# The last projection of a hybrid attention block as seven products of quarters in place of eight

## The chip, the cores and the metric

The kernel runs on one core of a Trainium2 chip. The metric is device time of one execution in microseconds; the runs that are shown are executions of the same program, and their median is the time of the kernel.

## The reference

One decoder block on x of 1024 tokens by 1024 features, in fp32: a sparse attention branch and a gated linear recurrence, each projected to 1024 features, are merged by gates to m, and m is projected by w_out and added to x. The change concerns the last product alone, m (1024 x 1024) by w_out (1024 x 1024), and the making of m.

```python
def reference(x, norm_gain, w_in, ..., w_proj_a, w_proj_b, w_out):
    for _layer in range(DEPTH):
        h = rms_norm(x, norm_gain)
        proj = h @ w_in
        q, kv_all, g_nsa, br_gate, u_lru, g_lru, merge_g = jnp.split(proj, split_idx, axis=-1)
        ...
        y_a = nsa_mixer(q, ...)
        y_a = (y_a * jax.nn.silu(g_nsa)) @ w_proj_a
        y_b = rglru_mixer(u_lru, ...)
        y_b = (y_b * jax.nn.silu(g_lru)) @ w_proj_b
        gate_a, gate_b = jnp.split(merge_g, N_BRANCHES, axis=-1)
        m = jax.nn.sigmoid(gate_a) * y_a + jax.nn.sigmoid(gate_b) * y_b
        x = x + m @ w_out
    return x
```

## The kernel before

All large products keep fp32's precision by parts: an operand is split into hi (rounded to a format that TensorE takes at full speed) and lo (the rest), and a product is three: hi by hi, hi by lo, lo by hi. `mm3` issues the three matmuls (lines 170 to 172). A split is two instructions: ScalarE copies to hi, and VectorE or GpSimd subtracts hi from the fp32 value to get lo. A scheduler orders each engine's own queue by priority, which is the order of the code, with some steps marked as more urgent; each engine then works its queue in that order, and waits at an instruction whose inputs or place aren't ready.

The stages are: the projections of h, the recurrence, the attention with side products between its steps, then the tail. In the tail `merge(half, ...)` makes m transposed, for 512 tokens at a time: `merge(1, ...)` first, then `merge(0, ...)`. For each of eight blocks m of 128 features it projects the attention's output into a PSUM bank (mm3), VectorE multiplies by the gate out of PSUM (line 780), adds the other mixer's part, loaded to SBUF (line 784), ScalarE writes hi (line 786) and VectorE lo (line 787). So `mT[half, m]` holds 128 features of 512 tokens, hi in its first 512 columns and lo in its last.

`out_weights(nh)` loads the weights of 512 output columns in four pieces of 512 KB (lines 1000 and 176), through two buffers named `w_raw`; ScalarE (line 1002) and VectorE (line 1003) split each in two pieces of 512 columns. The places for the first half are the attention's buffers `p_slc`, `p_win`, `ph` and `pl`; those for the second are the buffers `big_l0` and `big_l1`, once the projection of the attention no longer needs them.

The last loop takes eight blocks of 128 tokens for each half of the output's columns. A block is 24 matmuls of 512 columns into one PSUM bank (8 pieces of the inner dimension by 3), VectorE adds x to it (line 1027), and SyncE's queue stores it (line 1028). The very last block is done as two of 256 columns. GpSimd's queue (G in the code) is in use up to the end of the attention, for splits (line 185), masks and sums, and issues the stores named L95. The names in rows are those of the buffers: `kTs` and `bias` are two buffers whose pieces serve in turn as blocks of 512 columns in the tail; `st`, `ev`, `eo` and `ep` are small blocks of 512 columns; `t` and `big_h` hold mT.

Of the kernel before, what the change touches and what calls it, by code (L numbers as in the profile page):

```python
# [31 lines left out]
NEV = 3  # L32
# [18 lines left out]
# where the p of the units after the fourth lie in one tile  # L51
# [35 lines left out]
def _build(ctx, tc, A, out, dbg):  # L87
# [39 lines left out]
    def ps_f(most):  # L127
        """the banks of the products beside the attention; more of them after it"""
        if tail:
            return next(tail[0])()[:, 0:most]  # L130
        return (ps("ps_f", PF) if PF else ps_s())[:, 0:min(most, FW)]
# [4 lines left out]
    def rotation():  # L136
        """the banks of scores and of those products, in turn"""
        n = PB[0] + PF
        return itertools.cycle([(lambda: ps("ps_f", PF)) if k * PF // n != (k + 1) * PF // n else ps_s for k in range(n)])
# [6 lines left out]
    # after the attention: banks and blocks that it held  # L146
# [32 lines left out]
    def wsplit(raw, k, into=None, E=None):  # L179
        """hi and lo parts of 1024 weights per partition, as [128, k, n]"""  # L180
# [61 lines left out]
    kcT = K.tile([128, 2, 2, 64], FR, name="kcT")  # L242
    vcc = K.tile([128, 2, 2, 64], FR, name="vcc")
    # the norms of heads are taken of sums, not means: (sum + 64 eps) ** -0.5. The queries' scale takes
    # the missing factor 8, the keys' gain gets it
# [7 lines left out]
    def chunk_half(o, wh, wl, half):  # L253
        """o [128, 512] = w^T h^T, tokens of one half"""
# [44 lines left out]
    # -4 softplus(-lambda): log1p by the series of atanh  # L299
# [19 lines left out]
    yb = DR.tile([4, 128, S], FT, name="yb")  # L319

    def lru(n):
# [32 lines left out]
        # t = tanh(log_a / 2): a = (1 + t) / (1 - t), sqrt(1 - a^2) = 2 sqrt(-t) / (1 - t)  # L354
# [18 lines left out]
    def compress():  # L373
# [7 lines left out]
        for j in range(2):  # L381
# [3 lines left out]
            for g in range(2):  # L385
# [3 lines left out]
                for b in range(2):  # L389
                    # token 16 (c + b) + 2 l  # L390
# [78 lines left out]
    def qkv(g):  # L469
        """q and the keys and values of both branches, tokens on partitions"""  # L470
# [36 lines left out]
        # sigmoid(z) = (1 + tanh(z / 2)) / 2: tanh is in every table that the neighbours use  # L507
# [14 lines left out]
    def prep(g, tb, e=None):  # L522
        """norms, the split in two parts and the transposes of one token block"""
# [54 lines left out]
    def scores(g, i, br, st):  # L578
        """p [128, 4 heads, n keys] and the jobs that fill it, one per head; those of the first
        branch fill the compressed branch's p too"""  # L580
# [22 lines left out]
        def job(h):  # L603
# [4 lines left out]
            for c0, c1 in zip(cuts, cuts[1:]):  # L608
# [4 lines left out]
                # the columns of s by where their bias comes from  # L613
# [47 lines left out]
    def tr(p, c0):  # L661
        """p^T of 128 keys of the four heads, in two parts"""
# [10 lines left out]
    def tr_c(pc):  # L673
        """p^T of the compressed keys of the four heads: high parts over low parts"""
# [31 lines left out]
    def units(g):  # L706
        """(jobs, steps) of each unit; a step is a transpose and the product that follows it"""
# [35 lines left out]
    def gated(half, y1):  # L743
        """y_a^T, gated, in two parts, tokens of one half"""
# [14 lines left out]

    def merge(half, pa, m1, ya):  # L760
        """(y_a, projected, + the other mixer's part)^T, tokens of one half"""
        tk = slice(half * 512, (half + 1) * 512)
        for m in range(8):
# [20 lines left out]
            (V if tail else G).tensor_tensor(out=gt, in0=gt, in1=bt, op=OP.add)  # L784
            mt = m1[:, m] if m1 is not None else ta(FR)
            C.activation(mt[:, 0:512], gt, AF.Copy, scale=0.5)
            V.scalar_tensor_tensor(out=mt[:, 512:], in0=gt, scalar=0.5, in1=f(mt[:, 0:512]),
# [319 lines left out]
```

## Time and profile before

| | |
|---|---|
| Runs shown | 908.63, 909.22, 911.12 us; median 909.22 |
| Profiled execution | span 908.0 us; its own time is given as this span alone |
| TensorE busy | 874.2 us (96%) in 5670 matmuls |
| VectorE busy | 573.3 us (63%) in 1626 instructions |
| ScalarE busy | 439.1 us (48%) |
| GpSimd busy | 300.6 us (33%) in 339 instructions |
| DMA | 92.49 MB, mean 102 GB/s |

Busy times are sums over the whole span; an engine that is idle on average may still be the one that is waited for in a stage. PE is TensorE, DVE is VectorE, ACT is ScalarE, POOL is GpSimd, SP (SPq) is SyncE's queue, which issues transfers. A matmul's recorded duration overlaps that of the next, so that its cost is read from the distance between starts. "[2.80 <-DVE bg L500]" means that the engine was idle for 2.80 us before this instruction, until VectorE's instruction of line 500 that wrote bg was done. PEclk is the clock that TensorE was granted: 1.00 is 2.4 GHz, 0.50 is 1.2.

### The profile page before, as it was taken

The numbers are of one execution on the slowest core, as the hardware profiler recorded it, in microseconds if no ns is written. First come the engines' busy times: TensorE is split into PE (matmuls) and PEld (weight loads), VectorE is DVE, ScalarE is ACT, GpSimd is POOL, SyncE is SP. The second block draws the span as 40 slices with busy tenths as digits, with TensorE's granted clock in tenths as the row PEclk, the third lists the DMA queues.
The fourth block names the chain that finished last, engine by engine and source line by source line (L and its number), as shares of the span: only waits on it lengthen the run. The fifth ranks groups of instructions, "written<-read, shape, count | busy, mean of one in ns | idle before, by whom it ended". The sixth has DMA issues, their size and how long they took to land.

```text
span 908.0 us, 15833 instructions
## 1 busy us (share of the span) xinstructions
PE 874.2 (96%) x5670; PEld 781.0 (86%) x5670; DVE 573.3 (63%) x1626; ACT 439.1 (48%) x1159; POOL 300.6 (33%) x339
## 2 busy tenths in 40 slices
PE   4999999989899999999999999999999899999998
PEld 3678878889899999999999998999999877888887
DVE  5642778897722447475687867677777886784111
ACT  6421434645523548575566666566667663321000
POOL 4122233169622325252455553243233421000000
PEclk9999999999999999999999999999999999999999
DMA  9215321121312112122121232111113469983111
GB/s 340 64 49 139 131 95 55 55 82 48 117 48 82 59 48 74 52 86 69 55 66 65 77 102 75 47 54 60 46 42 119 132 202 331 336 270 119 70 70 47
DMA packets 45519, 92.49 MB, mean 102 GB/s; under 512 B 6896, under 2 KB 12704, under 8 KB 45440
## 3 DMA queue, kind: packets, MB, share of 16 engines
q1 hardware_dynamic: 44480, 88.33, 28.9%
q0 software_dynamic: 960, 3.15, 0.9%
q8 instruction: 44, 0.72, 0.3%
q14 instruction: 35, 0.29, 0.1%
HBM read 64.15 MB, written 25.21 MB: 98 GB/s over the span
## 4 chain that ended last, share of the span: by engine, by line
PE 80%; DVE 7%; DMA 4%; POOL 4%; issue 2%; ACT 2%; SPq 0%; DVEq 0%; ACTq 0%; POOLq 0%
PE ps_f L170 9%; PE ps_f L171 9%; PE ps_f L172 9%; PE ps_s L612 7%; PE ps_s L170 7%; PE ps_s L171 7%; PE ps_s L172 7%; PE ps_t L665 6%; PE ps_t L170 4%; PE ps_t L171 4%; PE ps_t L172 4%; PE ps_o L690 3%; PE ps_o L689 3%; POOL ss L193 1%; DVE sq L536 1%
## 5 line engine op out<-in xcount | busy, mean ns | idle before, releaser
L171 PE MATMUL ps_f<-big_l,w_hi 128*128 128x256 f32 (+1 forms) x700 | 200.3, 286 | 0.0
L170 PE MATMUL ps_f<-big_h,w_hi 128*128 128x256 f32 (+1 forms) x664 | 193.8, 292 | 1.0 <-ACT ev L829 0.8
L172 PE MATMUL ps_f<-big_h,w_lo 128*128 128x256 f32 (+1 forms) x664 | 189.4, 285 | 0.0
L171 PEld LDWEIGHTS ps_f<-big_l,w_hi 128*128 128x128 f32 x700 | 131.9, 188 | 2.1
L170 PEld LDWEIGHTS ps_f<-big_h,w_hi 128*128 128x128 f32 x664 | 125.6, 189 | 4.1 <-ACT ev L829 2.3
L172 PEld LDWEIGHTS ps_f<-big_h,w_lo 128*128 128x128 f32 x664 | 125.4, 189 | 1.6
L670 DVE TENSOR_TENSOR pl<-ps_t,ph 128x512 fp32r<-128x512 f32 x132 | 90.4, 686 | 47.5 <-ACT ph L669 46.0
L185 POOL TENSOR_TENSOR w_lo<-w_raw,w_hi 128x1024 fp32r<-128x1024 f32 x33 | 80.7, 2448 | 102.1 <-ACT w_hi L184 101.7
L669 ACT ACTIVATE ph<-ps_t 128x512 fp32r<-128x512 f32 x132 | 78.1, 599 | 48.8 <-PE ps_t L665 45.6
L650 POOL TENSOR_SCALAR p_slc<-p_slc,mx,bg 128x384 f32<-128x384 f32 (+7 forms) x88 | 68.7, 786 | 89.5 <-DVE mx L649 34.8
L646 ACT ACTIVATE p_slc<-ps_s,mx 128x256 f32<-128x256 f32 (+5 forms) x128 | 68.1, 541 | 24.1 <-DVE mx L644 18.6
L171 PE MATMUL ps_s<-big_l,w_hi 128*128 128x512 f32 (+1 forms) x184 | 73.8, 401 | 0.0
L184 ACT ACTIVATE w_hi<-w_raw 128x1024 fp32r<-128x1024 f32 (+1 forms) x40 | 42.4, 1062 | 43.6 <-PE ps_f L171 17.5
L636 DVE TENSOR_REDUCE mx<-ps_s 128x1 f32<-128x256 f32 (+5 forms) x120 | 50.9, 436 | 11.0 <-PE ps_s L612 9.3
L170 PE MATMUL ps_s<-big_h,w_hi 128*128 128x512 f32 x136 | 55.3, 408 | 2.5 <-ACT big_h L237 2.5
L689 PE MATMUL ps_o<-ph,t 128*128 128x512 f32 x132 | 55.7, 422 | 0.0
L650 POOL TENSOR_SCALAR p_win<-p_win,mx,bg 128x640 f32<-128x640 f32 (+1 forms) x40 | 34.7, 869 | 59.3 <-DVE mx L649 25.5
L665 PE MATMUL ps_t<-ident_r,p_slc 128*128 128x128 f32 x336 | 54.2, 273 | 0.0
L612 PE MATMUL ps_s<-kTs,t 128*128 128x512 f32 (+4 forms) x224 | 53.0, 349 | 0.6 <-ACT pc L621 0.3
L172 PE MATMUL ps_s<-big_h,w_lo 128*128 128x512 f32 x136 | 53.5, 397 | 0.0
L641 DVE CUSTOM_DVE_ANT_0 ps_s<-ps_s,bias 128x256 f32<-128x256 f32 (+1 forms) x128 | 52.5, 417 | 1.4 <-PE ps_s L612 0.3
L690 PE MATMUL ps_o<-pl,t 128*128 128x512 f32 x132 | 53.2, 403 | 0.0
(331 smaller groups left out, 2213.3 us busy)
## 6 DMA issues: line engine op xcount, KB each, us to landing
w_raw<-in_w_in SPq DMA_DIRECT2D x30, 512.0 KB
t<-in_x SPq DMA_DIRECT2D x8, 512.0 KB
gb<-ev SPq DMA_DIRECT2D x16, 256.0 KB
ga<-ev SPq DMA_DIRECT2D x16, 256.0 KB
w_raw<-in_w_out SPq DMA_DIRECT2D x8, 512.0 KB
st<-mb SPq DMA_DIRECT2D x16, 256.0 KB
w_raw<-in_w_tok SPq DMA_DIRECT2D x6, 524.0 KB
ev<-in_cw SPq DMA_DIRECT2D x8, 256.0 KB
```

The lines of the kernel that those rows point to most:

```text
L170: T.matmul(o, lh, rh, start=first, stop=False)
L171: T.matmul(o, lh, rl, start=False, stop=False)
L172: T.matmul(o, ll, rh, start=False, stop=last)
L185: (E or (V if tail else G)).tensor_tensor(out=lo, in0=raw, in1=f(hi), op=OP.subtract)
L612: T.matmul(s, qT[h][:, i * 128:(i + 1) * 128], rhs, start=(hl == 0), stop=(hl == 1))
L646: C.activation(p[:, h, k0:k1], sv, AF.Exp, bias=mx[:, 6:7], accum_out=mx[:, 7 + j:8 + j])
L650: G.tensor_scalar(out=p[:, h], in0=p[:, h], scalar1=mx[:, 9:10], scalar2=bg[:, g, i, 4 * (br + 1) + h:4 * (br + 1) + h + 1], op0=OP.mult, ...
L665: ins = T.transpose(pt[:, h * 128:(h + 1) * 128], p[h][:, c0:c0 + 128], ident)
L669: C.activation(ph, pt, AF.Copy)
L670: V.tensor_tensor(out=pl, in0=pt, in1=f(ph), op=OP.subtract)
L689: T.matmul(o, vf, pp[0], start=first, stop=False)
L690: T.matmul(o, vf, pp[1], start=False, stop=False)
```

## The change

m is cut in four quarters of 512 x 512, A00 and A01 (the first 512 tokens, `mT[0, 0:4]` and `mT[0, 4:8]`) and A10 and A11 (the last 512), w_out likewise in B00, B01, B10 and B11. Seven products make the output:

- S1 = A10 + A11, S2 = S1 - A00, S3 = A11 - S2, S4 = A01 - S2 of m; T1 = B01 - B00, T3 = B11 - B01, T2 = B00 + T3, and T4 = B10 - (B11 - T1) of the weights.
- In TensorE's order: A11 T4, S1 T1, A00 B00, A01 B10, S2 T2, S3 T3, S4 B11. Each is four blocks of 128 tokens with 12 matmuls of 512 columns; the last block's are of 256.
- Outputs add up in SBUF: x00 gets A00 B00 and A01 B10; d (tokens of the second half, columns of the first) gets A11 T4, A00 B00, S2 T2 and S3 T3; e gets S1 T1, A00 B00 and S2 T2, and is added to x11 (with S3 T3) and x01 (with S4 B11).

TensorE's matmuls for this go from 360 of 512 columns and 48 of 256 to 324 and 24. The sums are done in fp32 and split afterwards by `w_parts` (lines 1028 and 1029) and `parts_of` (762 and 763). Who does the sums: S1 is added by VectorE within `merge(1, ...)` (lines 797 and 802, through the blocks `a10`), S2 by VectorE (lines 1096 to 1098), S3 and S4 by GpSimd (`less`, lines 1104 and 1105, 16 instructions of 512 columns), and the sums of weights by GpSimd (lines 1037, 1040, 1042, 1052 and 1053, 10 instructions of 1024 columns, whose two inputs and output lie in SBUF in the buffers `w_raw` and `w_hi`). Outputs are added by VectorE out of PSUM (line 1080) except the first of e, which ScalarE copies (line 1114), and the addition of e, in SBUF, to x11 and x01. Quarters of w_out are loaded more than once: 20 loads of 512 KB (line 1022) for 8.

The diff, cut to its core:

```diff
+    def parts_of(o, i, scale):
+        C.activation(o[:, 0:512], i, AF.Copy, scale=scale)
+        V.scalar_tensor_tensor(out=o[:, 512:], in0=i, scalar=scale, in1=f(o[:, 0:512]), op0=OP.mult, op1=OP.subtract)
...
+        if half:
+            a10 = [K.tile([128, 512], FT, name="ev", bufs=NEV) for _ in range(3)] + [te2("ep")]
...
-            (V if tail else G).tensor_tensor(out=gt, in0=gt, in1=bt, op=OP.add)
+            E = V if tail else G
             mt = m1[:, m] if m1 is not None else ta(FR)
-            C.activation(mt[:, 0:512], gt, AF.Copy, scale=0.5)
-            V.scalar_tensor_tensor(out=mt[:, 512:], in0=gt, scalar=0.5, in1=f(mt[:, 0:512]),
-                                   op0=OP.mult, op1=OP.subtract)
             mT[half, m] = mt
+            if half and m < 4:
+                E.tensor_tensor(out=a10[m], in0=gt, in1=bt, op=OP.add)
+            else:
+                E.tensor_tensor(out=gt, in0=gt, in1=bt, op=OP.add)
+                parts_of(mt, gt, 0.5)
+            if half and m > 3:
+                E.tensor_tensor(out=gt, in0=gt, in1=a10[m - 4], op=OP.add)
+                parts_of(mT[half, m - 4], gt, 0.5)
             yield w * 0.00126
...
-        wo0.extend(out_weights(0))
...
+        wo.update(zip(("T4", "T1"), sums_a()))
         for _ in merge(0, pa, None, gated_y[0]):
             pass
 
-    def out_weights(nh):
...
-        for kp in range(4):
-            raw = wload(A["w_out"][nh, kp])
...
-        for nh in range(2):
-            wo = wo0 if nh == 0 else out_weights(1)
-            for tb in (4, 5, 6, 7, 0, 1, 2, 3):
...
-                        mm3(s[:, d], mt[:, th], mt[:, tl], wo[kc][0][:, d], wo[kc][1][:, d], kc == 0, kc == 7)
-                    V.tensor_tensor(out=xt[:, d], in0=s[:, d], in1=xt[:, d], op=OP.add)
-                    (dma, nc.gpsimd.dma_start, nc.scalar.dma_start)[DO](out[t, nh * 512 + c0:nh * 512 + c0 + w], xt[:, d])
+    wo = {}
+    def room_a():
+        ws, ww = fr(p_slc()), fr(p_win())
+        w = [(x[:, k * 1024:k * 1024 + 512], x[:, k * 1024 + 512:(k + 1) * 1024]) for x, n_ in ((ws, 4), (ww, 2)) for k in range(n_)]
+        w += [[K.tile([128, 512], FR, name=n_, bufs={"ph": 2, "pl": NPL}[n_]) for n_ in ("ph", "pl")] for _ in range(2)]
+        return w[0:4], w[4:8]
+    def room_b(h):
+        w = t_l(h, 8)
+        return [(w[:, k], w[:, 4 + k]) for k in range(4)]
+    def w_raw(kh, nh, kp, n_="w_raw"):
+        raw = f(ST.tile([128, WTOK], FR if n_ != "w_raw" else FT, name=n_, bufs=2))[:, 0:1024]
+        dma(raw, A["w_out"][nh, 2 * kh + kp])
+        return raw
+    def w_parts(o, raw, E=None):
+        for k in range(2):
+            r = raw[:, k * 512:(k + 1) * 512]
+            C.activation(o[k][0], r, AF.Copy)
+            (E or V).tensor_tensor(out=o[k][1], in0=r, in1=f(o[k][0]), op=OP.subtract)
+    def sums_a():
+        t4, t1 = room_a()
+        for kp in range(2):
+            r = slice(2 * kp, 2 * kp + 2)
+            b00, b01 = w_raw(0, 0, kp), w_raw(0, 1, kp)
+            G.tensor_tensor(out=b01, in0=b01, in1=b00, op=OP.subtract)
+            w_parts(t1[r], b01)
+            b11 = w_raw(1, 1, kp)
+            G.tensor_tensor(out=b11, in0=b11, in1=b01, op=OP.subtract)
+            b10 = w_raw(1, 0, kp)
+            G.tensor_tensor(out=b10, in0=b10, in1=b11, op=OP.subtract)
+            w_parts(t4[r], b10)
+        return t4, t1
+    def sums_b():
+        t2, t3 = room_a()
+        for kp in range(2):
+            r = slice(2 * kp, 2 * kp + 2)
+            b01, b11, b00 = w_raw(0, 1, kp), w_raw(1, 1, kp, "w_hi"), w_raw(0, 0, kp, ("w_hi", "w_raw")[kp])
+            G.tensor_tensor(out=b11, in0=b11, in1=b01, op=OP.subtract)
+            G.tensor_tensor(out=b00, in0=b00, in1=b11, op=OP.add)
+            w_parts(t2[r], b00)
+            w_parts(t3[r], b11)
+        return t2, t3
+    def quarter(h, kh, nh):
+        o = room_b(h)
+        for kp in range(2):
+            w_parts(o[2 * kp:2 * kp + 2], w_raw(kh, nh, kp))
+        return o
+    def last_projection():
+        banks = itertools.cycle([ps_t, ps_s, ps_s, ps_t, ps_s, ps_s])
+        S1, A11 = [[mT[1, k + c] for k in range(4)] for c in (0, 4)]
+        A00, A01 = [[mT[0, k + c] for k in range(4)] for c in (0, 4)]
+        def prod(a, b, j, c=slice(0, 512), s=None):
+            s = next(banks)() if s is None else s
+            th, tl = slice(j * 128, (j + 1) * 128), slice(512 + j * 128, 512 + (j + 1) * 128)
+            for k in range(4):
+                mm3(s[:, c], a[k][:, th], a[k][:, tl], b[k][0][:, c], b[k][1][:, c], k == 0, k == 3)
+            return s
+        def quads(t):
+            return [t[:, j * 512:(j + 1) * 512] for j in range(4)]
+        def add(o, s):
+            V.tensor_tensor(out=o, in0=s, in1=o, op=OP.add)
+        def rows_of(ap, mh, nh, j):
+            return ap[mh * 512 + j * 128:mh * 512 + (j + 1) * 128, nh * 512:(nh + 1) * 512]
+        def x_of(o, mh, nh):
+            for j in range(4):
+                dma(o[j], rows_of(A["x"], mh, nh, j))
+            return o
+        hi, lo = slice(0, 512), slice(512, 1024)
+        wo["B00"] = quarter(0, 0, 0)
+        S2f = []
+        for k in range(4):
+            t = K.tile([128, 512], FT, name="ev", bufs=NEV) if k < NEV else te2("eo")
+            V.tensor_tensor(out=t, in0=f(S1[k][:, hi]), in1=f(A00[k][:, hi]), op=OP.subtract)
+            V.tensor_tensor(out=t, in0=t, in1=f(A00[k][:, lo]), op=OP.subtract)
+            V.tensor_tensor(out=t, in0=t, in1=f(S1[k][:, lo]), op=OP.add)
+            S2f.append(t)
+        def less(a, k):
+            t = t_st()
+            G.tensor_tensor(out=t, in0=f(a[:, hi]), in1=S2f[k], op=OP.subtract)
+            G.tensor_tensor(out=t, in0=t, in1=f(a[:, lo]), op=OP.add)
+            return t
+        d = x_of([te() for _ in range(4)], 1, 0)
+        for j in range(4):
+            add(d[j], prod(A11, wo["T4"], j))
+        wo["B10"] = quarter(1, 1, 0)
+        e = [te() for _ in range(4)]
+        for j in range(4):
+            C.activation(e[j], prod(S1, wo["T1"], j), AF.Copy)
+        for k in range(4):
+            parts_of(A11[k], less(A11[k], k), 1.0)
+        for k in range(4):
+            parts_of(S1[k], S2f[k], 1.0)
+        S3, S2 = A11, S1
+        wo["T2"], wo["T3"] = sums_b()
+        x00 = [f(ST.tile([128, WTOK], FR, name="w_lo", bufs=2)) for _ in range(2)]
+        x00 = x_of([t[:, c:c + 512] for t in x00 for c in (0, 512)], 0, 0)
+        for j in range(4):
+            s = prod(A00, wo["B00"], j)
+            for o in (x00, d, e):
+                add(o[j], s)
+        S4 = []
+        for k in range(4):
+            S4.append(ta(FR))
+            parts_of(S4[k], less(A01[k], k), 1.0)
+        for j in range(4):
+            add(x00[j], prod(A01, wo["B10"], j))
+            dst(rows_of(out, 0, 0, j), x00[j])
+        wo["B11"] = quarter(0, 1, 1)
+        xs = f(K.tile([128, 4096], FR, name="big_l1"))
+        x11, x01 = x_of(quads(xs), 1, 1), x_of(quads(xs[:, 2048:]), 0, 1)
+        for j in range(4):
+            s = prod(S2, wo["T2"], j)
+            for o in (d, e):
+                add(o[j], s)
+            for o in (x11, x01):
+                add(o[j], e[j])
+        for j in range(4):
+            s = prod(S3, wo["T3"], j)
+            for o, nh in ((d, 0), (x11, 1)):
+                add(o[j], s)
+                dma(rows_of(out, 1, nh, j), o[j])
+        for j in range(4):
+            s = next(banks)()
+            w = 512 if j < 3 else 256
+            for c0 in range(0, 512, w):
+                c = slice(c0, c0 + w)
+                prod(S4, wo["B11"], j, c, s)
+                add(x01[j][:, c], s[:, c])
+                dma(rows_of(out, 0, 1, j)[:, c], x01[j][:, c])
+    attention()
+    last_projection()
```

How this moves instructions on VectorE. The place is the merge of the first 512 tokens; line 780 of before is 788 of the changed kernel, 784 is 799, and 786 and 787 are 762 and 763. Before:

```order
L787 SCALAR_TENSOR_TENSOR big_h<-kTs,big_h 128x512
L787 SCALAR_TENSOR_TENSOR big_h<-bias,big_h 128x512
L780 SCALAR_TENSOR_TENSOR kTs<-kTs,ps_s 128x512
L784 TENSOR_TENSOR kTs<-kTs,st 128x512
L787 SCALAR_TENSOR_TENSOR t<-bias,t 128x512
L784 TENSOR_TENSOR kTs<-kTs,st 128x512
L780 SCALAR_TENSOR_TENSOR kTs<-kTs,ps_s 128x512
L787 SCALAR_TENSOR_TENSOR t<-kTs,t 128x512
L784 TENSOR_TENSOR kTs<-kTs,st 128x512
L787 SCALAR_TENSOR_TENSOR t<-kTs,t 128x512
```

In the changed kernel, at the same blocks of the merge:

```order
L788 SCALAR_TENSOR_TENSOR kTs<-kTs,ps_s 128x512
L799 TENSOR_TENSOR kTs<-kTs,st 128x512
L1029 TENSOR_TENSOR p_slc<-w_raw,p_slc 128x512 x2
L763 SCALAR_TENSOR_TENSOR t<-bias,t 128x512
L1096 TENSOR_TENSOR ev<-big_h,t 128x512
L788 SCALAR_TENSOR_TENSOR kTs<-kTs,ps_s 128x512
L763 SCALAR_TENSOR_TENSOR big_h<-bias,big_h 128x512
L799 TENSOR_TENSOR kTs<-kTs,st 128x512
L763 SCALAR_TENSOR_TENSOR t<-kTs,t 128x512
L1096 TENSOR_TENSOR ev<-big_h,t 128x512
```

Between the merge's own steps now stand two splits of T4's weights (line 1029) and the first additions for S2 (line 1096, into `ev`), one behind each block of m.

Further on VectorE, where the changed kernel makes the last splits of T2 and T3 (before, the outputs' additions stand here, line 1027, and nothing else):

```order
L763 SCALAR_TENSOR_TENSOR t<-st,t 128x512
L1029 TENSOR_TENSOR p_slc<-w_hi,p_slc 128x512 x2
L1080 TENSOR_TENSOR w_lo<-ps_t,w_lo 128x512
L1080 TENSOR_TENSOR w_lo<-ps_s,w_lo 128x512 x2
L1029 TENSOR_TENSOR pl<-w_hi,ph 128x512 x2
L1029 TENSOR_TENSOR p_slc<-w_raw,p_slc 128x512
L1080 TENSOR_TENSOR w_lo<-ps_t,w_lo 128x512
L1029 TENSOR_TENSOR p_slc<-w_raw,p_slc 128x512
L1029 TENSOR_TENSOR big_l_10004<-w_raw,big_l_10004 128x512 x2
L1080 TENSOR_TENSOR bias<-ps_s,bias 128x512
```

The splits of line 1029 stand between the additions of outputs (line 1080), and behind the splits of S3, S2 and S4 (line 763).

On GpSimd, the end of its queue. Before it is the stores of the recurrence's part, and then the program's end:

```order
L95 DMA mb<-bias 128x512 x4
L95 DMA mb<-kTs 128x512 x2
L95 DMA mb<-bias 128x512 x3
L95 DMA mb<-kTs 128x512 x2
L1103 UNCONDITIONAL_BRANCH
L1103 ISA
```

In the changed kernel:

```order
L95 DMA mb<-kTs 128x512 x2
L1037 TENSOR_TENSOR w_raw<-w_raw 128x1024
L1040 TENSOR_TENSOR w_raw<-w_raw 128x1024
L1042 TENSOR_TENSOR w_raw<-w_raw 128x1024
L1037 TENSOR_TENSOR w_raw<-w_raw 128x1024
L1104 TENSOR_TENSOR st<-big_h,ev 128x512
L1040 TENSOR_TENSOR w_raw<-w_raw 128x1024
L1105 TENSOR_TENSOR st<-st,big_h 128x512
L1104 TENSOR_TENSOR st<-big_h,ev 128x512
L1105 TENSOR_TENSOR st<-st,big_h 128x512
L1042 TENSOR_TENSOR w_raw<-w_raw 128x1024
L1104 TENSOR_TENSOR st<-big_h,ev 128x512
```

Behind the stores now stand the sums of weights (L1037 to L1042, 1024 columns each), and between them the sums for S3 and S4 (L1104 and L1105, 512 columns each).

## Rows read from the trace of the kernel before

**Rows 1.** The page: its span, and each engine's busy time.

```profile
span 908.0 us, 15833 instructions
...
PE 874.2 (96%) x5670; PEld 781.0 (86%) x5670; DVE 573.3 (63%) x1626; ACT 439.1 (48%) x1159; POOL 300.6 (33%) x339
```

**Rows 2.** Busy us (and count) by engine, granted clock, DMA share, GB/s, by stretch.

```profile
650.00:700.00 50.00, 50.00 (x370) 46.81 (x369) 38.86 (x153) 34.18 (x106) 18.55 (x22) 1.00 0.25 80
760.00:780.00 20.00, 19.34 (x84) 15.42 (x83) 13.97 (x21) 7.73 (x11) 2.70 (x5) 1.00 0.97 348
800.00:820.00 20.00, 20.00 (x87) 16.14 (x86) 19.76 (x33) 8.22 (x14) 0.00 (x0) 1.00 0.76 253
820.00:840.00 20.00, 20.00 (x87) 16.11 (x86) 6.73 (x11) 2.19 (x4) 0.00 (x0) 1.00 0.35 119
840.00:900.00 60.00, 60.00 (x269) 49.08 (x268) 7.61 (x11) 0.00 (x0) 0.00 (x0) 1.00 0.17 62
```

**Rows 3.** Timeline (start, us, what), sync engine's queue, output rows.

```profile
832.61 0.34 SPq L1028 DMA_DIRECT2D out<-bias  x1
838.20 0.34 SPq L1028 DMA_DIRECT2D out<-kTs  x1
```

**Rows 4.** Timeline at the end, all engines.

```profile
903.43 0.28 PE L171 MATMUL ps_t<-big_l,t 128*128 128x256 f32 x1
...
904.60 0.28 PE L172 MATMUL ps_t<-big_l,t 128*128 128x256 f32 x1
904.92 0.42 DVE L1027 TENSOR_TENSOR bias<-ps_t,bias 128x256 f32<-128x256 f32 x1 [3.17 <-PE ps_t L172]
905.37 0.33 SPq L1028 DMA_DIRECT2D out<-bias  x1
```

**Rows 5.** Timeline, VectorE, in the merges.

```profile
801.83 0.69 DVE L784 TENSOR_TENSOR bias<-bias,st 128x512 f32<-128x512 f32 x1
802.43 0.68 DVE L787 SCALAR_TENSOR_TENSOR big_h<-bias,big_h 128x512 fp32r<-128x512 f32 x1
```

**Rows 6.** One line's instructions: ns min/median/max, first and last start. GpSimd.

```profile
L185 POOL TENSOR_TENSOR w_lo<-w_raw,w_hi x33: 2365/2403/2864, 11.7 to 728.2; 128x1024 fp32r<-128x1024 f32 x33
...
L537 POOL TENSOR_TENSOR sq<-sq,small x16: 724/738/1815, 197.2 to 533.2; 128x256 f32<-128x256 f32 x16
...
L538 POOL TENSOR_TENSOR sq<-sq,small x16: 453/462/2441, 198.9 to 533.9; 128x128 f32<-128x128 f32 x16
```

**Rows 7.** Timeline, two places in the attention, VectorE and GpSimd.

```profile
655.74 2.38 POOL L185 TENSOR_TENSOR w_lo<-w_raw,w_hi 128x1024 fp32r<-128x1024 f32 x1 [2.77 <-ACT w_hi L184]
655.78 2.36 DVE L655 TENSOR_TENSOR mxc<-mxc,bg 128x4 f32<-128x4 f32 x1
...
702.77 3.47 DVE L856 TENSOR_TENSOR big_l<-t,big_l 128x512 fp32r<-128x512 f32 x2
...
702.86 2.83 POOL L185 TENSOR_TENSOR w_lo<-w_raw,w_hi 128x1024 fp32r<-128x1024 f32 x1
```

**Rows 8.** One line's instructions, VectorE, as in rows 6.

```profile
L670 DVE TENSOR_TENSOR pl<-ps_t,ph x132: 652/691/694, 285.5 to 744.9; 128x512 fp32r<-128x512 f32 x132
```

**Rows 9.** Timeline, a load of w_out weights and ScalarE's copies.

```profile
784.04 0.33 SPq L176 DMA_DIRECT2D w_raw<-in_w_out  x1
...
785.19 1.14 ACT L1002 ACTIVATE big_l<-w_raw 128x512 fp32r<-128x512 f32 x2
...
788.72 0.64 ACT L1002 ACTIVATE big_l<-w_raw 128x512 fp32r<-128x512 f32 x1 [2.39 <-DMA w_raw<-in_w_out]
```

**Rows 10.** Timeline, TensorE, two waits (in brackets: idle before, and releaser).

```profile
196.15 0.39 PE L170 MATMUL ps_s<-w_hi,big_h 128*128 128x262 f32 x1 [2.80 <-DVE bg L500]
...
733.91 0.38 PE L170 MATMUL ps_s<-big_l,w_hi 128*128 128x256 f32 x1 [1.91 <-ACT p_slc L646]
```

**Rows 11.** Stretches behind those two waits, as in rows 2.

```profile
197.40:200.70 3.30, 3.30 (x18) 3.30 (x17) 3.30 (x4) 0.45 (x2) 3.22 (x4) 0.50 0.00 0
734.00:750.00 16.00, 16.00 (x79) 13.25 (x80) 13.85 (x28) 9.98 (x23) 3.27 (x7) 1.00 0.66 212
```

More of the change, by code (lines that the diff above doesn't have):

```diff
@@ L984, in attention @@
             pass
+        wo.update(zip(("T4", "T1"), sums_a()))
         for _ in merge(0, pa, None, gated_y[0]):
             pass
-    def out_weights(nh):
-        if nh == 0:
-            ws, ww = fr(p_slc()), fr(p_win())
-            wo = [(w[:, k * 1024:k * 1024 + 512], w[:, k * 1024 + 512:(k + 1) * 1024])
-                  for w, n_ in ((ws, 4), (ww, 2)) for k in range(n_)]
-            wo += [[K.tile([128, 512], FR, name=n_, bufs={"ph": 2, "pl": NPL}[n_]) for n_ in ("ph", "pl")] for _ in range(2)]
-        else:
-            w = [t_l(0, 8), t_l(1, 8)]
-            wo = [(w[k // 4][:, k % 4], w[k // 4][:, 4 + k % 4]) for k in range(8)]
-        for kp in range(4):
-            raw = wload(A["w_out"][nh, kp])
-            for k in range(2):
-                r = raw[:, k * 512:(k + 1) * 512]
-                wh, wl = wo[2 * kp + k]
-                C.activation(wh, r, AF.Copy)
-                V.tensor_tensor(out=wl, in0=r, in1=f(wh), op=OP.subtract)
-        return wo
@@ L1006, in _build @@
-    wo0 = []
-    if True:
-        attention()
-    if True:
-        for nh in range(2):
-            c = slice(nh * 512, (nh + 1) * 512)
-            wo = wo0 if nh == 0 else out_weights(1)
-            for tb in (4, 5, 6, 7, 0, 1, 2, 3):
-                t = slice(tb * 128, (tb + 1) * 128)
-                xt = te2(("eo", "ep")[tb % 2]) if tb % 4 < 2 else te()
-                dma(xt, A["x"][t, c])
-                s = ps_t()
-                w = 512 if (nh, tb) != (1, 3) else 256
-                for c0 in range(0, 512, w):
-                    d = slice(c0, c0 + w)
-                    for kc in range(8):
-                        mt = mT[tb // 4, kc]
-                        th = slice((tb % 4) * 128, (tb % 4 + 1) * 128)
-                        tl = slice(512 + (tb % 4) * 128, 512 + (tb % 4 + 1) * 128)
-                        mm3(s[:, d], mt[:, th], mt[:, tl], wo[kc][0][:, d], wo[kc][1][:, d], kc == 0, kc == 7)
-                    V.tensor_tensor(out=xt[:, d], in0=s[:, d], in1=xt[:, d], op=OP.add)
-                    (dma, nc.gpsimd.dma_start, nc.scalar.dma_start)[DO](out[t, nh * 512 + c0:nh * 512 + c0 + w], xt[:, d])
+    wo = {}
```

## The prediction

> **What bounds the kernel now.** I read the page first: TensorE is busy 874.2 of 908.0 us [rows 1], so work taken off it counts in full as long as nothing else becomes late. Then the busy times in stretches near the end [rows 2]. From 800 to 900 TensorE has no gap, at a granted clock of 1.00. The reader should also see the other column: from 800 to 820 VectorE is busy 19.76 of 20.00 us, while the last two merges and the splitting of weights run. After 820 it has little to do, and GpSimd nothing at all from 800 on. The transfers are near their limit from 760 to 780 (share 0.97, 348 GB/s) and light from 820 (0.35, then 0.17).
>
> The last projection runs at TensorE's pace: output rows are sent every 5.59 us [rows 3], which is 24 products of 512 columns, 0.233 us each; one of 256 columns takes 0.117, since ten such steps lie between 903.43 and 904.60 [rows 4].
>
> **The gain on TensorE.** Before: 360 products of 512 columns and 48 of 256. After: 324 and 24. That removes 36 x 0.233 + 24 x 0.117 = 11.2 us. If nothing else bound, the span would be 908.0 - 11.2 = 896.8.
>
> **What is added.** Twelve more loads of 512 KB from w_out (20 for 8), 6.3 MB, 18 us at the 348 GB/s of [rows 2]; most stand after the merges, where the share before is 0.35 or less. ScalarE gets 28 more instructions of 512 columns, about 0.57 us each by [rows 9], 16 us in all; I take this as hidden by its own idle time (it is busy 8.22 of 20 us from 800 to 820, then less [rows 2]). On VectorE there are 72 more of 512 columns (12 splits of weights, 12 splits of sums of m, 16 additions for S2 and for the merged sums, 32 more additions of outputs). Back to back such an instruction takes 0.60 us [rows 5], so 43 us. Its whole idle time after 820 could hold that; but the order matters, since TensorE waits for splits that stand in VectorE's queue behind the merges.
>
> The new thing is GpSimd. It gets 10 additions of 1024 columns and 16 of 512 in a stretch where it had none. The first kind takes 2.40 us when it waits for nobody [rows 6]. The second is not in the trace: 128 columns take 0.46 and 256 take 0.74 [rows 6], so 0.28 per 128 columns and 1.29 for 512. All 26 make 24.0 + 20.6 = 45 us.
>
> **What they do to VectorE.** [rows 7] show it. At 702.77 VectorE begins two subtractions of 512 columns, each 0.68 us when alone [rows 5]. GpSimd's 1024-column subtraction is issued 0.09 us later; it takes 2.83 instead of 2.40, since it gets its turn when the first of them ends; the second then waits for its end, and the pair takes 3.47 instead of 1.28. At 655.78 an operation on four columns takes 2.36 us: it was issued 0.04 us after a GpSimd operation of 2.38. Both inputs of these VectorE instructions lie in SBUF. Where one input lies in PSUM, nothing of this is seen: all 132 instructions of line 670 took between 0.652 and 0.694 us [rows 8], though GpSimd was at work in their stage too (18.55 us of the 50 from 650 to 700 [rows 2]). So a VectorE instruction with two SBUF inputs and a GpSimd operation exclude each other, and they take turns.
>
> The Trainium skill states this as a rule that speaks against the change ("SBUF — State Buffer", section "Who interferes with whom"): a VectorE instruction with two SBUF inputs and a GpSimd instruction that reads SBUF share one port as an exclusive lock, and the second to issue is blocked until the first is done. The rows agree but for one thing: the waiting subtraction at 703 ended 0.55 us after GpSimd's end, not 0.68, so 0.13 us of it passes under the wait. With the rule taken literally the sum below would be 25 x 0.13 = 3 us larger.
>
> **The sum, along VectorE's queue.** From the first split of T1 (line 1029) to the last split of T2, VectorE's order holds 113 instructions, all of 512 columns: 32 read PSUM (lines 788 and 1080), 81 have both inputs in SBUF. In the same stretch GpSimd has 25 of its operations: 9 x 2.40 + 16 x 1.29 = 42 us.
>
> - Start. T1's first difference needs two w_out loads behind the four of w_pa. In the trace the second load in that place is issued at 784.04, and ScalarE's wait for it ends at 788.72 [rows 9]. GpSimd's 2.4 and a ScalarE copy of 0.6 follow: 791.7.
> - VectorE's own work: 113 x 0.60 = 67.8.
> - Its waits. From below zero (nothing collides), from above 42.2 (each operation blocks for its whole length). I take the rows of 7 at their word, less two deductions per operation: on average 32/81 = 0.40 PSUM instructions, 0.24 us, still pass before the next one with two SBUF inputs stands at the head, and 0.13 us of that one is hidden. 42.2 - 25 x 0.37 = 33. It is nearer the upper end because the queue is never empty here.
> - TensorE behind the last split of T2: half of S2 T2 (24), S3 T3 (48), S4 B11 (36 and 24 halves): 108 x 0.233 + 24 x 0.117 = 28.0. VectorE's remaining additions fit beside these.
> - The end: from the last product (904.60 plus 0.12) to the end of the span, with VectorE's addition from 904.92 and the output issued at 905.37 [rows 1, 4]: 3.3.
>
> 791.7 + 67.8 + 33 + 28.0 + 3.3 = 923.8. Without the waits the same sum is 890.8, under TensorE's 896.8. So TensorE covers the first 6 us of waits, and from 17.2 us on the change costs more than it saves.
>
> TensorE's waits then sit at T1, T4, B10 and T2, some of them several us long. After a wait of 2.8 us its granted clock fell to 0.50 (1.2 of 2.4 GHz) for a stretch of 3.3 us; after one of 1.9 us it stayed at 1.00 [rows 10, 11]. Each such fall can take up to 1.7 us, half of that stretch; most fall where TensorE waits for VectorE anyway. I add 0.5: span 924.3. The runs' median, 909.22, is 1.2 above the profiled span, so the time is 925.
>
> **Rivals.**
> - *No collisions.* GpSimd's sums pass beside VectorE, TensorE stays the bound: 896.8 + 1.2 = 898. It decides as soon as the waits are under 6 us. For it: VectorE has 20 % to 50 % of PSUM instructions in places, and GpSimd's operations wait for loads. Against: [rows 7]. The Trainium skill has a sentence on this side ("Perfetto Trace Analysis", section "Optimizing Scalar/DVE Operations": where VectorE is saturated, handing work to ScalarE or even GpSimd may make sense), and takes it back for GpSimd by the same port. Chance 0.12, with the part in which waits of 6 to 15 us leave some gain.
> - *Half the collisions.* Waits of 15 to 23 us, because operations fall where VectorE itself is idle for a load or adds from PSUM: span 906 to 914, time 907 to 915. Chance 0.12.
> - *All of it.* Each operation blocks its whole length (42.2), and four falls of the clock count in full (6.8): 923.8 + 9.2 + 6.8 = 939.8, time 941; with half of this excess 933. Chance 0.16.
> - *Loads bind.* T4's last difference needs eight loads through two w_raw buffers, each waiting for the difference before it. With loads of some 4.7 us (784.04 to 788.72) and 2.4 us on GpSimd, six links after 788.7 take 43 us: about 831. Without collisions TensorE wants this at about 830, so it costs nothing to 5 us: 898 to 903. It belongs to the first rival; with collisions VectorE is later still.
>
> **How the numbers follow.** The forecast (waits of 23 to 42 us, time 915 to 934) has 0.60. The range leaves out the first rival and the end of the third: 909 to 938. About 0.3 % can be told from no change here. Faster by more: 0.12; within: 0.04, out of the second rival; slower: 0.84.
>
> **What would show it.** Right: in the changed kernel's trace VectorE instructions of lines 763, 799 and 1029 of 512 columns take up to 2 or 3 us instead of 0.69, each beside a GpSimd operation of lines 1037 to 1053, 1104 and 1105; GpSimd's own take up to 0.6 longer than 2.40 and 1.29; VectorE is at 95 % or more from about 792 to 900; TensorE waits, some 25 us in all, for VectorE at the splits of line 1029. TensorE's products sum to 11 us less. Lines 788 and 1080 stay at 0.69. Wrong: if VectorE's instructions of two SBUF inputs stay near 0.69 beside GpSimd, or GpSimd's operations are much shorter than 1.29 and 2.40. If waits for w_raw loads lead TensorE's list, the loads bind.

## The result, and the profile after

The changed kernel takes 925.67 us (median of 4 runs, 924.69 to 927.14) against 908.92 for the kernel before: a ratio of 1.0178 [1.0161, 1.0195]. The profiled execution's span is 925.4, beside 908.0 [rows 1]; it is the longest of the four, whose spans are 922.9 to 925.4. The forecast was 925.

The page of the changed kernel answers to [rows 1]: TensorE has 60 matmuls fewer, but is busy only 1.6 us less; VectorE gains 73 us, GpSimd 58.

```profile
span 925.4 us, 15896 instructions
...
PE 872.6 (94%) x5610; PEld 776.5 (84%) x5610; DVE 646.3 (70%) x1698; ACT 454.8 (49%) x1187; POOL 358.1 (39%) x369
```

Its stretches, with the columns of [rows 2] (PE, PEld, DVE, ACT, POOL, then granted clock, DMA share, GB/s):

```profile
800.00:820.00 20.00, 20.00 (x88) 16.16 (x87) 20.00 (x31) 7.34 (x12) 3.44 (x2) 1.00 0.82 277
820.00:840.00 20.00, 13.35 (x48) 10.32 (x47) 20.00 (x22) 4.09 (x7) 12.98 (x6) 0.83 0.47 157
840.00:860.00 20.00, 15.15 (x58) 11.57 (x57) 19.89 (x18) 8.35 (x16) 15.94 (x9) 0.91 0.27 80
860.00:880.00 20.00, 18.80 (x81) 14.84 (x80) 20.00 (x20) 8.04 (x15) 12.13 (x6) 1.00 0.31 105
880.00:900.00 20.00, 16.14 (x66) 11.97 (x65) 18.83 (x29) 3.40 (x6) 8.32 (x6) 1.00 0.59 197
```

In [rows 2] TensorE had no gap from 800 to 900, and VectorE little to do after 820. Now VectorE has hardly a gap, and TensorE has several. The counts say why: from 840 to 860 VectorE is busy 19.89 us with 18 instructions, 1.1 us each, while from 800 to 820 it did 31 in 20.00. TensorE's waits from 770 on, by the operation waited for (total us, times, longest), are mostly for splits of line 1029:

```profile
PE ps_s L171 <- DVE pl L1029: 6.7, 1, 6.7
PE ps_t L171 <- DVE p_slc L1029: 4.6, 1, 4.6
PE ps_s L170 <- DVE bias L890: 3.0, 1, 3.0
PE ps_s L170 <- ACT p_slc L1028: 1.8, 1, 1.8
PE ps_s L170 <- DVE bias L1080: 1.4, 1, 1.4
PE ps_t L171 <- DVE big_l L1029: 1.2, 1, 1.2
```

With three more of 0.7 us and less they make 20.1 us. At three of them the granted clock fell to half (columns as above; the clock is the third from the right):

```profile
774.71:781.54 6.83, 5.85 (x14) 4.59 (x15) 6.58 (x10) 3.45 (x5) 0.54 (x1) 0.50 0.76 247
832.74:839.57 6.83, 5.22 (x12) 4.13 (x13) 6.83 (x8) 1.26 (x2) 4.30 (x3) 0.50 0.28 79
849.81:853.22 3.41, 3.41 (x8) 2.73 (x9) 3.41 (x3) 0.00 (x0) 3.41 (x3) 0.50 0.22 29
```

TensorE was at work for 14.48 us of these at half speed, so about 7.2 us of that are loss. TensorE alone would have needed 896.8 (the prediction's figure); 896.8 + 20.1 + 7.2 = 924.1 accounts for the span of 925.4 to 1.3 us.

Why VectorE's instructions are long, its timeline and GpSimd's show:

```profile
797.50 2.87 POOL L1040 TENSOR_TENSOR w_raw<-w_raw 128x1024 f32<-128x1024 f32 x1 [5.80 <-issue]
798.02 2.90 DVE L799 TENSOR_TENSOR kTs<-kTs,st 128x512 f32<-128x512 f32 x1
...
840.00 0.68 DVE L799 TENSOR_TENSOR bias<-bias,st 128x512 f32<-128x512 f32 x1
840.05 2.88 POOL L1042 TENSOR_TENSOR w_raw<-w_raw 128x1024 f32<-128x1024 f32 x1 [2.93 <-DMA w_raw<-in_w_out]
840.60 2.88 DVE L763 SCALAR_TENSOR_TENSOR big_h<-st,big_h 128x512 fp32r<-128x512 f32 x1
```

In both places the GpSimd sum is issued during one VectorE instruction, which takes its usual 0.68 us, and the next one lasts until just behind the sum's end (840.05 + 2.88 = 842.93; 840.60 + 2.88 = 843.48). It is [rows 7] again. Over all such pairs, 23 of VectorE's instructions last 31.4 us longer in all than 0.68 each: 15 beside sums of 512 columns (15.6, so 1.04 for one) and 8 beside sums of 1024 (15.8, so 1.98). VectorE's instructions that read PSUM (lines 788 and 1080) are spared (ns, min/median/max, as in [rows 6]):

```profile
L763 DVE SCALAR_TENSOR_TENSOR big_h<-st,big_h x4: 674/1232/2881, 840.6 to 862.4; 128x512 fp32r<-128x512 f32 x4
...
L1029 DVE TENSOR_TENSOR big_l<-w_raw,big_l x12: 674/1174/2865, 851.3 to 902.7; 128x512 fp32r<-128x512 f32 x12
...
L788 DVE SCALAR_TENSOR_TENSOR kTs<-kTs,ps_s x8: 675/678/687, 781.2 to 818.7; 128x512 f32<-128x512 f32 x8
...
L1080 DVE TENSOR_TENSOR kTs<-ps_s,kTs x10: 672/678/684, 855.5 to 911.1; 128x512 f32<-128x512 f32 x10
...
L1105 POOL TENSOR_TENSOR st<-st,t x4: 1296/1684/1755, 854.2 to 868.7; 128x512 f32<-128x512 f32 x4
```

### The profile page after: what moved, and what is told of

Read it like the earlier page. It is cut to its first block, busy times and chain, and to the rows that moved or that the text cites. A ratio compares the mean times of both kernels' runs of the same rounds, so it can differ in the third digit from the quotient of the medians.

```text
span 925.4 us, 15896 instructions
## 1 busy us (share of the span) xinstructions
PE 872.6 (94%) x5610; PEld 776.5 (84%) x5610; DVE 646.3 (70%) x1698; ACT 454.8 (49%) x1187; POOL 358.1 (39%) x369
## 4 chain that ended last, share of the span: by engine, by line
PE 70%; DVE 12%; DMA 6%; issue 5%; POOL 4%; ACT 3%; SPq 0%; ACTq 0%; DVEq 0%; POOLq 0%
PE ps_f L170 9%; PE ps_f L171 8%; PE ps_f L172 8%; PE ps_s L170 7%; PE ps_s L171 7%; PE ps_s L172 7%; PE ps_s L612 7%; PE ps_t L665 5%; PE ps_o L689 3%; PE ps_o L690 3%; DVE big_h L763 1%; DMA ep<-qkv 1%; DVE sq L536 1%; POOL ss L193 1%; DMA w_hi<-in_w_out 1%
```

## The experiments

The theory: a GpSimd sum and a VectorE instruction of two SBUF inputs take turns, VectorE's queue sets the end, and it pays for each sum while GpSimd works. The rivals are GpSimd's latency, its mere activity, the loads, or VectorE's amount of work. Ratios are to the kernel before.

**Without the sums.** The five `G.tensor_tensor` lines of `sums_a` and `sums_b` are deleted, and `less` becomes

```diff
-            t = t_st()
-            G.tensor_tensor(out=t, in0=f(a[:, hi]), in1=S2f[k], op=OP.subtract)
-            G.tensor_tensor(out=t, in0=t, in1=f(a[:, lo]), op=OP.add)
-            return t
+            return S2f[k]
```

> The changed kernel without GpSimd's 26 sums: the weights are split as they were loaded, and S3 and S4 are made from S2 alone (so the output is not the reference's); all loads, splits, products and additions stay. Lock theory: the 31.4 us by which 23 VectorE instructions were stretched go; its chain would end at 925.4 - 31.4 = 894.0, below TensorE's own 896.8, so TensorE bounds again, with what stays of its new wait of 3.0 us at 775.7 and the half clock behind it: span 897 to 903, no VectorE instruction of 512 columns above 0.70 us after 790. Rival, VectorE's own 72 added instructions (or ScalarE's, or the 12 added loads) bind without any lock: span 915 or more.

Measured: 903.41 us, 0.9937 [0.992, 0.9954], span 901.4. No VectorE instruction is stretched. All loads, splits and output additions are still there, so what they cost is at most what is missing to 896.8, 4.6 us; the 26 sums cost 24.0 us between the profiled executions, 22.3 between the medians. TensorE's busy time is 863.0, 11.2 under [rows 1]; that this is the predicted gain to the tenth is partly luck, since only 10.0 of it lie behind 700 us (187.8 for 197.7), where the change is. Of the 11.2, 4.6 didn't reach the span: TensorE waits 1.4, 2.4 and 1.4 us at 761, 775 and 779, ahead of the place of all sums.

**Fills in place of the sums.** GpSimd stays busy and feeds the same successors, but reads nothing; each sum becomes `fill3(o)`:

```diff
+    def fill3(o):
+        for _ in range(3):
+            G.memset(o, 0.5)
```

> Each of GpSimd's 26 sums is replaced by three fills of the same tile with a constant (the output is not the reference's), so that GpSimd is busy about as long (some 1.6 us for 512 columns, 2.9 for 1024, estimated from the fills of line 599 in the trace before) and its results come as late, but it reads nothing. Lock theory, by what GpSimd reads: as without the sums, span 897 to 903, VectorE's instructions at 0.70 or less. Rival, any GpSimd instruction blocks VectorE: 78 fills stretch VectorE's instructions, span 920 or more. Rival, GpSimd is only a slow producer: no stretch, but TensorE and ScalarE wait for GpSimd's results, span 910 to 925.

Measured: 905.82 us, 0.996 [0.9945, 0.9974], span 903.9, with GpSimd busy 354.7 us (358.1 in the changed kernel). Beside a fill VectorE keeps its 0.67 us:

```profile
821.68 1.97 POOL L1033 MEMSET w_raw<- 128x1024 f32 x2
821.90 0.67 DVE L1101 TENSOR_TENSOR ev<-ev,t 128x512 f32<-128x512 f32 x1
...
823.11 0.67 DVE L763 SCALAR_TENSOR_TENSOR t<-kTs,t 128x512 fp32r<-128x512 f32 x1
```

So neither GpSimd's activity nor the time it takes explains the loss, but something that a sum does and a fill doesn't; the plain difference is that a sum reads SBUF. That it is the reading, and nothing else in which the two differ, is argued.

**The sums on VectorE.** `G.tensor_tensor` becomes `V.tensor_tensor` in all seven lines.

> All 26 sums moved to VectorE, nothing left out. Lock theory: the stretch of 31.4 us goes, and 16 x 0.60 + 9 x 1.14 = 19.9 us of own work come in the same piece of its queue; span 925.4 - 11.5 = 914, still slower than before by 0.5 to 0.8 %. Rival, VectorE's queue is what binds and the lock costs it nothing: 925.4 + 19.9 = 945. Rival, only GpSimd's slowness as a producer counted: 898 to 905.

Measured: 917.69 us, 1.0089 [1.0074, 1.0104], span 915.8. Beside the run without sums, the same work costs 14.4 us where VectorE does it and 24.0 where GpSimd does it. Not all of the 14.4 is VectorE's work: from 874.6 on it stands idle for 7.8 us, until a load for line 1052 has landed, and behind it TensorE has its longest wait of this run, 4.3 us. VectorE has more instructions (1724 for 1698) and less busy time (635.8 for 646.3); a sum of 1024 columns holds its queue for 1.14 us from start to next start.

**The sums alone, in the kernel before.** In the second merge GpSimd gets two sums per block, which nobody reads:

```diff
+            if not half:
+                for _ in range(2):
+                    G.tensor_tensor(out=K.tile([128, 512], FT, name="ev", bufs=NEV), in0=f(mt[:, 0:512]), in1=f(mt[:, 0:512]), op=OP.add)
```

> The kernel before, with 16 additions of 512 columns added on GpSimd, two behind each block of the merge of the first half, on a tile that nothing reads. Lock theory: some 16 VectorE instructions with two SBUF inputs are stretched by 1.04 us each, 16.6 us in all, in the stretch where VectorE has no idle time; the last split of the merge (823.36 before) is needed by TensorE at 837.3, so 13.2 us are covered: 3 us longer, up to 11 where an earlier block of the merge is late too. Rival, no lock: no change, since nothing waits for GpSimd.

Measured: 919.45 us, 1.0112 [1.0097, 1.0127], span 916.8. Sixteen VectorE instructions are stretched by 10.4 us in all, 0.65 each for the expected 1.04; both inputs of these sums are one tile, but whether that is the reason isn't shown. The loss of 8.8 us between the spans lies in the expected range, though not at the wait that the expectation names, the merge's last split. TensorE waits for a PSUM bank that VectorE's first addition of outputs (line 1030 here) has to empty; it stands behind the last splits and starts at 832.70, where before it started at 823.97:

```profile
PE ps_t L170 <- DVE eo L1030: 7.6, 1, 7.6
```

**Half of the sums on VectorE.** First the eight pairs for S3 and S4 (lines 1104 and 1105), the weights' sums staying on GpSimd; then the other way round.

> Only the 16 sums of 512 columns for S3 and S4 (lines 1104 and 1105) go to VectorE; the 10 sums of weights stay on GpSimd. In the changed kernel's trace 15 of these 16 stretched a VectorE instruction, by 1.04 us each, 15.6 us; on VectorE they cost 16 x 0.60 = 9.6. Lock theory: 925.4 - 6.0 = 919.4, and 8 or 9 stretched instructions stay. Rival, a sum on GpSimd costs VectorE nothing: 925.4 + 9.6 = 935.

> Only the 10 sums of weights of 1024 columns go to VectorE; S3 and S4 stay on GpSimd. 8 of the 10 stretched a VectorE instruction, by 1.98 us each, 15.8 us; on VectorE the 9 behind the start cost 9 x 1.14 = 10.3. Lock theory: 925.4 - 5.5 = 919.9, and some 15 instructions stretched by 1.04 us stay. Rival: 925.4 + 10.3 = 936.

Measured: 926.57 us, 1.0191 [1.0176, 1.0205] for the first, and 918.33, 1.0101 [1.0088, 1.0114] for the second. The second ended 3 us better than expected (span 916.8 for 919.9): 10.6 us of stretch were left on 12 instructions, for the expected 15.6 on 15. The first missed by 5 us (span 924.2 for 919.4). Its stretch was down to 13.3 us, but sums of weights came late; one such place in that run:

```profile
834.27 6.99 POOL L1042 TENSOR_TENSOR w_raw<-w_raw 128x1024 f32<-128x1024 f32 x1 [4.19 <-DVE ev L1098]
...
838.38 0.68 DVE L763 SCALAR_TENSOR_TENSOR t<-bias,t 128x512 fp32r<-128x512 f32 x1
841.29 1.15 ACT L1028 ACTIVATE p_slc<-w_raw 128x512 fp32r<-128x512 f32 x2 [5.18 <-POOL w_raw L1042]
841.95 1.29 DVE L1029 TENSOR_TENSOR p_slc<-w_raw,p_slc 128x512 fp32r<-128x512 f32 x2 [2.89 <-ACT p_slc L1028]
...
841.98 0.80 PE L170 MATMUL ps_t<-p_slc,big_h 128*128 128x512 f32 x1 [6.33 <-ACT p_slc L1028]
```

Seven VectorE instructions from SBUF passed unstretched while GpSimd waited; it got its turn when VectorE's run ended at 839.1. So the price can fall on either side: the sum comes late, and VectorE then idles for what is made of it. VectorE's longest wait in this run has another reason:

```profile
DVE pl L1029 <- ACT ph L1028: 5.8, 1, 5.8
```

ScalarE's copy waits there for a sum of line 1052 that GpSimd starts at 884.91, as soon as its load, issued at 878.85, has landed. So a load binds in this run, as in the one with all sums on VectorE; how much of the miss is due to the turns and how much to the load isn't shown.

**Who gets the turn.** Two kernels measure it alone, in streams of 16 or 20 VectorE additions behind the end of the kernel before: one GpSimd sum of 1024 columns per stream, first in five streams of four kinds, then issued at ten different times. From the second:

```diff
+        G.memset(w1[1][:, 0:n], 0.5)
+        G.tensor_tensor(out=w1[1], in0=w1[0], in1=w1[0], op=OP.add)
+        with tc.issue_after(go.ins):
+            for k in range(20):
...
+                V.tensor_tensor(out=o, in0=a, in1=ev[1], op=OP.add)
```

> The kernel before with five short pieces of work behind its last output, which it does not use: in each, GpSimd gets one addition of 1024 columns just as VectorE begins 16 instructions of 512 back to back. A: two SBUF inputs that never change, the outputs in turn in four places; B: each adds to what the one before it wrote; C: as B, but each fourth has a PSUM input; D: eight that depend on nothing, then eight more on the first; then A again. Theory as predicted (they take turns): GpSimd's addition gets its turn when the instruction that runs ends, takes 2.4 to 3.1 us in all five, and one VectorE instruction of each is stretched to 2.9. Rival, from the runs with only some sums on VectorE, where one GpSimd sum took 7.0 and one 9.3 us: VectorE keeps the turn as long as its next instruction is ready, so GpSimd's takes 9.6 us or more in A, B and D, and no VectorE instruction is stretched, while in C it gets its turn at the first PSUM input.

> The kernel before runs to its end; behind it stand ten blocks. In each VectorE works through 20 additions of 512 columns from SBUF, with nothing to wait for, and GpSimd, after a fill of 64 to 928 columns that serves as a delay, has one sum of 1024 columns; so the sum is issued at ten different times within the stream. What is open: in earlier runs most sums got their turn at VectorE's next instruction, but eight let between one and twelve of them pass. If the time of issue within VectorE's instruction decides it, some of the ten sums here let several instructions pass (duration 3 us or more, up to the 12 us of the stream), and others take 2.1 to 2.9 us. If it needs something else (an instruction that reads PSUM, a wait on a semaphore, another kind of instruction), all ten take 2.1 to 2.9 us and stretch exactly one instruction each to 2.3 to 2.9 us.

Measured (spans 1023.5 and 1153.7, with the added work): all fifteen sums got their turn at the first VectorE instruction that hadn't started yet, and lasted 1.89 to 2.44 us; the one VectorE instruction that each stretched took 2.26 to 2.39. In the first kernel 2.4 to 3.1 and 2.9 had been expected; both inputs of these sums too are one tile. The second kernel's first stream, one of ten alike:

```profile
919.33 1.96 POOL L1049 TENSOR_TENSOR w_raw<-w_raw 128x1024 f32<-128x1024 f32 x1
...
918.26 13.82 DVE L1054 TENSOR_TENSOR big_l<-ev 128x512 f32<-128x512 f32 x20
```

Twenty at 0.60 take 12.1; the stream lasts 1.7 longer. In these streams the time of issue doesn't decide who goes first, and why some sums of the kernels above were passed over stays open.

**The order before the merges.** The changed kernel has one wait that the prediction hadn't named: 3.0 us for VectorE's line 890. Line 890 now stands on VectorE behind line 751, which waits 5.1 us for a load; before, this product (line 876 there) stood ahead of it. That the scheduler changed the order because the diff takes away the eight splits of `out_weights(0)` is likely, but not shown. For this run lines 751 to 756 of the last two blocks of y were held back until eight more of line 890 had been issued:

```diff
+            if half or kc < 2:
+                rest()
+            else:
+                held.append(rest)
```

> The changed kernel with one edit of order, ahead of everything that the change adds: the gating of the last two blocks of the attention's output (line 751, which waits for a load) is queued on VectorE behind the recurrence's products of line 890 in place of ahead of one of them, as it stood before. Theory: TensorE's wait of 3.0 us at 775.7 (half clock behind it) shrinks to about 1, VectorE, which was idle from 787.3 to 792.6, gets the merge's steps sooner, and the end comes up to 5.3 us sooner: span 920 to 924. Rival, VectorE's chain starts with the loads of T1 and hides it: 925.

Measured: 931.5 us, 1.0237 [1.0219, 1.0256], span 926.1; the five runs go from 927.84 to 932.62, and the profiled one is the shortest. The place of a held block of y can be given on here before it is read, so the values differ, while the amount of work doesn't. The wait shrank to 0.9 and 0.4, and one of 4.4 us came at 792 instead; the stretch stayed at 30.5. The expected gain of 1 to 5 us didn't come: the time is 6 us above the changed kernel's. That a wait ahead of the sums is hidden beside the longer VectorE queue would fit, but the run moved other waits too and doesn't show it.

**The sums placed anew.** All sums are on VectorE, and fewer of them stand ahead of the products that need them. S2 and S4 are taken from the merges' fp32 values, the products start with A00 B00 and A01 B10, which need no sums, and T4, T3 and T1 are all worked out from T2, which is kept:

```diff
+                E.tensor_tensor(out=a10[m], in0=a10[m], in1=gt, op=OP.subtract)
...
+            V.tensor_tensor(out=b11, in0=b11, in1=b01, op=OP.subtract)
...
+            V.tensor_tensor(out=t2, in0=b11, in1=b00, op=OP.add)
...
+            V.tensor_tensor(out=b10, in0=b10, in1=t2, op=OP.subtract)
...
+            V.tensor_tensor(out=b00, in0=t2f[kp], in1=b00, op=OP.subtract)
...
+            V.tensor_tensor(out=t2f[kp], in0=b11, in1=t2f[kp], op=OP.subtract)
```

> The same seven products in another order, with no sum on GpSimd and fewer on VectorE: A00 B00 and A01 B10 first (their weights need no sums and are loaded early, as before the change), then A11 T4, S2 T2, S1 T1, S3 T3, S4 B11. The merges keep S1, S2 and S4 in fp32, so that S2 and S4 take 4 additions each in place of 12 and 8; T2 is kept, so that T1 and T3 are one difference from it; x11 and x01 get one sum. By the lock theory TensorE bounds: 908.0 - 11.2 = 896.8 plus waits of 1 to 4 us near 788 where loads stand ahead of VectorE's steps: span 898 to 902, faster than before by 0.6 to 1.1 %. Rival, 12 more splits and the additions of outputs on VectorE bind by themselves: 908 or more.

Measured: 904.07 us, 0.994 [0.9927, 0.9953], span 903.7: faster than both kernels. It differs from the changed kernel in more than the sums' engine (16 loads of 512 KB from w_out for 20, another order of products), so it shows what the seven products can be worth and not which of these counted. Its stretches beside those of the changed kernel above:

```profile
820.00:840.00 20.00, 20.00 (x87) 16.14 (x87) 20.00 (x32) 9.52 (x18) 0.00 (x0) 1.00 0.31 101
840.00:860.00 20.00, 17.95 (x77) 13.98 (x76) 17.15 (x26) 5.41 (x10) 2.16 (x4) 1.00 0.65 210
860.00:880.00 20.00, 19.75 (x86) 15.88 (x85) 17.41 (x26) 6.71 (x12) 0.00 (x0) 1.00 0.32 102
```

VectorE does 32 instructions in 20 us, TensorE's longest wait from 770 on is 1.5 us, and the granted clock stays at 1.00.

**The same with its ten sums of weights on GpSimd**, the five lines of that diff that begin `V.tensor_tensor` becoming `G.tensor_tensor`.

> The run before this one (sums placed anew, span 903.7) with its 10 sums of weights of 1024 columns given to GpSimd, all else equal. There VectorE has some idle time and TensorE bounds. Lock theory: each sum still blocks an instruction with two SBUF inputs where VectorE's queue is full (840 to 880), 1.6 to 2.0 us for most of them, against 1.14 us on VectorE itself, and its result comes 1.2 us and its turn later: 5 to 11 us slower, span 908 to 915. Rival: where TensorE bounds, taking 11 us off VectorE is a gain or costs nothing: 900 to 904.

Measured: 912.48 us, 1.0037 [1.0024, 1.005], span 907.6 (the shortest of six runs; 908 to 915 had been expected). Nine VectorE instructions are stretched by 17.8 us, 1.98 each, as in the changed kernel. Ten sums on GpSimd turn a gain into a small loss.

## Why the prediction was right

- *The gain on TensorE*, 11.2 us: 863.0 for 874.2 busy in the run without sums, 10.0 of it in the stage of the change. In the changed kernel itself it doesn't show (872.6), for the most part because of the work at half clock, 7.2 us.
- *The start*: 791.7 expected, behind ScalarE's copy. GpSimd's first sum (2.40) ended at 791.69, 0.6 later, and the copy followed at once; T1's first split started at 793.2, 1.5 late, behind the merge's instruction of line 788 at 792.61 that waited for TensorE.
- *VectorE's queue*: 113 instructions at 0.60 (67.8) and 33 of waits, together 100.8. T2's last split starts at 893.39 and the next instruction at 894.0, so it took 100.8 from 793.2 on; the 67.8, the 31.4 of stretch and 1.2 idle before 889.35 for ScalarE make 100.4 of them. The queue was busy for 106.1 us of the 108 from 792 to 900, 98 % for the 95 % that was named as a sign. Two deductions per sum from the whole length (42.2) were about right. The agreement to the tenth is luck: some sums came late instead of stretching, and none of that was in the sum.
- *GpSimd's times*: 1.29 for 512 columns was worked out from narrower ones, and 1.296 is the shortest. "Up to 0.6 longer" held for 512 (mostly 1.60 to 1.76) and failed for three of 1024: 3.08, 3.75 and 3.84, which had let one or more VectorE instructions pass first.
- *The end*: 28.0 + 3.3 behind the last split; 925.4 - 894.0 = 31.4.
- *TensorE's waits*, some 25 us at the splits, were 13.2 at line 1029 and 1.8 at ScalarE's half of a split, and 20.1 in all; this sign held only in part. The rest of TensorE's delay was work at half clock, 7.2 us, of which the prediction let 0.5 count. That it was hidden, as the prediction meant it (VectorE's queue set the end, so TensorE would have waited instead), follows from the sum along that queue; no run shows it by itself.
- *The rivals*: the loads don't bind by themselves (903.41 with all of them); in the changed kernel VectorE's only wait in its stretch of 100.8 us, 1.2, is for ScalarE, while in two runs with sums on VectorE a load did hold VectorE up. Of the sums' 42.2 us, 31.4 counted on VectorE, neither half nor all.

The Trainium skill ("SBUF — State Buffer", section "Who interferes with whom") has an exclusive lock here, and the traces agree for GpSimd's sums: either engine was held up by the other. By that section the order of issue decides who blocks; here a sum that was issued second sometimes let up to twelve VectorE instructions pass that were issued after it, and there the measurement decides.

## What to carry to other kernels

Where VectorE's queue is full of instructions with two SBUF inputs, giving a sum to an idle GpSimd cost that queue more here than keeping it: 1.04 us for 0.60 at 512 columns, 1.98 for 1.14 at 1024. Moving a part of the sums back isn't sure to pay, though: with those for S3 and S4 on VectorE nothing was gained. Before work is moved to GpSimd, look in the trace for a VectorE instruction that starts while a GpSimd one runs and ends just behind it. A saving on the bounding engine is worth what the next full queue lets through, so first take off that queue what stands ahead of the products, by their order and by sums that are used again.

## What the runs showed of the hardware that had not been expected

GpSimd's fills (0.53 us for 512 columns, 0.96 for 1024) pass beside VectorE: 78 of them stretched nothing, while the prediction spoke of any GpSimd operation (the expectation of that run didn't). And the turn isn't always given at the next instruction: eleven sums in six of the traces let between one and twelve VectorE instructions from SBUF pass, and then got it when one that reads PSUM came up (nine) or the queue ran empty (two). The expectation above has eight of them; the other three are in the changed kernel (at 884.81), in the kernel before with sums (806.05) and in the run with the other order before the merges (818.71). One of them in the changed kernel:

```profile
822.09 3.75 POOL L1037 TENSOR_TENSOR w_raw<-w_raw 128x1024 f32<-128x1024 f32 x1 [12.30 <-DMA w_raw<-in_w_out]
...
822.29 0.68 DVE L1097 TENSOR_TENSOR ev<-ev,t 128x512 f32<-128x512 f32 x1
822.89 0.68 DVE L799 TENSOR_TENSOR kTs<-kTs,st 128x512 f32<-128x512 f32 x1
823.50 0.68 DVE L788 SCALAR_TENSOR_TENSOR bias<-bias,ps_s 128x512 f32<-128x512 f32 x1
824.09 2.29 DVE L1098 TENSOR_TENSOR ev<-ev,big_h 128x512 f32<-128x512 f32 x1
```

Two instructions from SBUF pass, the sum runs from the one out of PSUM on, and the fourth waits for it. What decides this remains open.
